# A skewness kernel: cubes written over their squares in PSUM, the sums of GpSimd's cubes in four steps, and a shorter last act for VectorE

**Chip and metric.** One core of a Trainium2 chip. The metric is the device time of one execution in microseconds (us). The engines are TensorE (PE, with its weight loads as PEld), VectorE (DVE), ScalarE (ACT), GpSimd (POOL) and SyncE (SP, which issues the loads).

## The reference

```python
x = randn(1024, 8192)            # float32
mean = np.mean(x, axis=-1, keepdims=True)
std = np.std(x, axis=-1, keepdims=True)
z = (x - mean) / (std + 1e-8)
return np.mean(z ** 3, axis=-1)
```

For each of 1024 rows the kernel needs three sums over 8192 columns: of x, of its squares, and of its cubes. The skewness follows from these.

## The kernel before

Eight blocks of 128 rows pass through, each cut into units of columns (33.55 MB of input in all, 31 loads). For each unit, PE transposes chunks of 128 columns and adds them up in PSUM (`tp`), which gives the sum of x; ACT squares and sums the squares on the way; DVE multiplies the squares by x and sums the cubes. In three places GpSimd takes the multiplication instead. The operation used there gives no sum with it, so the sum of its cubes goes round by PE (transposes into `gps`), ACT (a copy to `gsb`), PE (a product with ones, `p3`) and ACT (a copy into `s3u`).

```python
POOL = {(6, 0): 1024, (7, 0): 1024, (7, 2): 1024}   # (block, unit): columns for GpSimd
EARLY_AT = (7, 3)                                   # where blocks 0 to 6 are finished
...
tp = psum1.tile([P, P], FP, tag="tp", name="tp")
misc = psum1.tile([P, 2 * P], FP, tag="misc", name="misc")
gps = misc[:, 0:P]                    # transposes of GpSimd's cubes
s1ps = misc[:, P : P + NB]            # the mean of each block
...
def sum_cubes(sq, col):               # a generator: one step in each of several units
    for c in range(n):
        nc.tensor.matmul(out=gps, lhsT=sq[:, c * P : (c + 1) * P], rhs=ident, ..., is_transpose=True)
    yield
    nc.scalar.copy(out=gsb, in_=gps)
    p3 = misc[:, P + NB : P + NB + 1]
    nc.tensor.matmul(out=p3, lhsT=gsb, rhs=ones, start=True, stop=True)
    yield
    nc.scalar.copy(out=s3u[:, col : col + 1], in_=p3)
...
for each unit:                        # i counts the units
    # PE: transposes of xt into tp
    if last_unit:
        nc.scalar.copy(out=tsb, in_=tp)
    for s, e, on_pool in _plan(b, k):
        act(out=sq, in_=xt[:, s:e], func=AF.Square, scale=s_scale, accum_out=s2u[:, j : j + 1])
        if on_pool:
            g.tensor_tensor(out=sq, in0=sq, in1=xt[:, s:e], op=ALU.mult)
            steps = sum_cubes(sq, j)
            later += [(i + 3, steps), (i + 4, steps), (i + 5, steps)]
        else:
            nc.vector.scalar_tensor_tensor(
                out=cube[:, 0 : e - s] if (b, k) >= PSUM_FROM else sq,   # cube: one buffer in SBUF
                in0=sq, scalar=1.0, in1=xt[:, s:e],
                op0=ALU.mult, op1=ALU.mult, accum_out=s3u[:, j : j + 1])
    for at, steps in later:           # the steps that are due in this unit
        if at == i:
            next(steps, None)
    if (b, k) == EARLY_AT:
        nc.scalar.copy(out=m1a, in_=s1ps[:, 0:F])
        close_first_blocks()
# after the units of a block: tsb <- tp on ACT (but in the last block), then on PE
    nc.tensor.matmul(out=s1ps[:, b : b + 1], lhsT=tsb, rhs=onesn, start=True, stop=True)
...
# the end of the last block
g.tensor_tensor(out=m2, in0=m2p, in1=s2u[:, j - 1 : j], op=ALU.add)
act(out=m1sq, in_=p1, func=AF.Square)                        # p1: the mean, in PSUM
g.tensor_tensor(out=var, in0=m2, in1=m1sq, op=ALU.subtract)
g.tensor_tensor(out=rr, in0=var, in1=expo[:, 0:1], op=ALU.pow)
act(out=nm1, in_=p1, func=AF.Copy, scale=-3.0)
act(out=v3, in_=m1sq, func=AF.Identity, scale=1.0 / 3.0, bias=var)
nc.vector.tensor_reduce(out=num, in_=s3u[:, L * K : L * K + n_sl[L]], axis=X_AXIS, op=ALU.add)
nc.vector.scalar_tensor_tensor(out=num, in0=v3, scalar=nm1, in1=num, op0=ALU.mult, op1=ALU.add)
nc.vector.tensor_tensor(out=skew[:, L:NB], in0=num, in1=rr, op=ALU.mult)
```

In the last steps `v3` is the variance plus a third of the squared mean, `rr` the variance to the power -1.5, and `num` the numerator of the skewness. From unit 3 of block 5 on (`PSUM_FROM`) the squares lie in PSUM, in three buffers (`psq`); before that, squares and cubes share four buffers in SBUF (`sq`).

## Time and profile before

| | before |
|---|---|
| time, median of 3 runs | 93.35 us (93.28 to 93.52) |
| profiled span | 91.6 us |
| busy: PE, DVE, ACT, POOL | 75%, 78%, 76%, 12% |
| loads | 33.55 MB, 366 GB/s over the span |

A line of the timeline gives start and duration in us, engine, source line, operation, output and input, shape, count, and in brackets the idle time before it with what ended that; a line `...` marks lines left out. A square or cube that also sums (`accum_out`) is followed by a short instruction that reads out the sum, its accumulator read. Three moments: when the load stream thins out (from about 81.5 us; the last load lands near 84), when PE's last transpose ends (87.16), and when DVE's last step ends (89.36).

### The profile page before, as it was taken

Reading aid. Unit: us, or ns where it says so; the run is one execution under the profiler, and the core shown is the slowest. Engines: PE = TensorE matmul, PEld = TensorE weight load, DVE = VectorE, ACT = ScalarE, POOL = GpSimd, SP = SyncE. Lnnn points to the kernel's source line nnn. Section 1 sums busy time; section 2 is a strip of 40 time slices with the busy share of each in tenths; the row PEclk is TensorE's granted clock in tenths of the full one; section 3 lists DMA queues with packets and bytes.
Section 4 is the critical chain, followed back from the end, with each engine's and each line's share of the span. In section 5 each row is a group of like instructions: output and inputs, shape, how many; then the busy total and the mean of one; then the engine's idle time right before and its main releaser. Section 6 shows DMA issues by size and latency. Waiting matters only on the chain.

```text
span 91.6 us, 1528 instructions
## 1 busy us (share of the span) xinstructions
PE 68.9 (75%) x558; PEld 64.8 (71%) x558; DVE 71.7 (78%) x94; ACT 70.1 (76%) x117; POOL 11.3 (12%) x20
## 2 busy tenths in 40 slices
PE   0002999896983999899939796979787998977920
PEld 0003999795972999799939685969676997967910
DVE  1000498989899398999999999998999999668970
ACT  6003969696982959999949896999978998969750
POOL 3000000000000000000000000000072002998040
PEclk9999999999999569999999999999999999999999
DMA  4899999999999999999999999999999999980000
GB/s 114 329 422 422 436 436 443 408 451 422 436 415 429 416 427 429 424 405 443 417 430 404 432 423 414 416 403 422 420 415 404 411 406 409 393 319 35 0 0 2
DMA packets 4615, 33.64 MB, mean 367 GB/s; under 512 B 641, under 2 KB 769, under 8 KB 2817
## 3 DMA queue, kind: packets, MB, share of 16 engines
q1 hardware_dynamic: 4608, 33.56, 88.5%
q8 instruction: 4, 0.07, 0.3%
q14 instruction: 3, 0.02, 0.0%
HBM read 33.55 MB, written 0.00 MB: 366 GB/s over the span
## 4 chain that ended last, share of the span: by engine, by line
DMA 65%; PE 18%; ACT 5%; DVE 5%; issue 2%; SPq 1%; POOL 0%; ACTq 0%; DVEq 0%
DMA x<-in_x_dram 65%; PE tp L163 14%; DVE sq L186 5%; PE misc L140 3%; ACT sq L177 2%; ACT psq L177 2%; SPq L159 1%; PE misc L147 1%; PE misc L206 0%; ACT v_l L219 0%; ACT tsb L205 0%; DVE num_l L221 0%; POOL var_l L216 0%; POOL m_l L214 0%; ACT nm1a L127 0%
## 5 line engine op out<-in xcount | busy, mean ns | idle before, releaser
L163 PE MATMUL tp<-ident,x 128*128 128x128 f32 x512 | 63.8, 285 | 14.4 <-DMA x<-in_x_dram 14.4
L163 PEld LDWEIGHTS tp<-ident,x 128*128 128x128 f32 x512 | 60.1, 149 | 16.1 <-issue 8.5
L186 DVE SCALAR_TENSOR_TENSOR sq<-sq,x 128x2048 f32<-128x2048 f32 (+7 forms) x26 | 52.4, 2064 | 13.0 <-ACT sq L177 13.0
L177 ACT ACTIVATE sq<-x 128x2048 f32<-128x2048 f32 (+7 forms) x26 | 44.8, 1725 | 14.0 <-DMA x<-in_x_dram 14.0
L186 DVE SCALAR_TENSOR_TENSOR cube<-psq,x 128x1024 f32<-128x1024 f32 (+4 forms) x17 | 18.2, 1068 | 3.5 <-ACT psq L177 2.4
L182 POOL TENSOR_TENSOR gsq<-gsq,x 128x1024 f32<-128x1024 f32 x3 | 7.1, 2375 | 73.6 <-ACT gsq L177 73.6
L177 ACT ACTIVATE psq<-x 128x1024 f32<-128x1024 f32 (+4 forms) x17 | 15.2, 893 | 0.8 <-DMA x<-in_x_dram 0.8
L206 PEld LDWEIGHTS misc<-onesn,tsb 128*128 128x128 f32 x16 | 2.4, 188 | 5.5 <-ACT tsb L205 4.9
L206 PE MATMUL misc<-onesn,tsb 128*128 128x1 f32 x16 | 3.1, 260 | 3.6 <-ACT tsb L205 3.2
L177 ACT ACTIVATION_READ_ACCUMULATOR sq<-x 128x1 f32 x26 | 4.8, 185 | 0.0
L177 ACT ACTIVATION_READ_ACCUMULATOR psq<-x 128x1 f32 x17 | 3.2, 189 | 0.0
L177 ACT ACTIVATE gsq<-x 128x1024 f32<-128x1024 f32 x3 | 3.2, 1054 | 0.0
L140 PE MATMUL misc<-ident,gsq 128*128 128x128 f32 x24 | 3.1, 274 | 0.0
L205 ACT COPY tsb<-tp 128x128 f32<-128x128 f32 x7 | 1.8, 256 | 1.3 <-PE tp L163 1.1
L140 PEld LDWEIGHTS misc<-ident,gsq 128*128 128x128 f32 x24 | 2.7, 141 | 0.1
L186 DVE DVE_READ_ACCUMULATOR sq<-sq,x 128x1 f32 x26 | 2.2, 83 | 0.0
L147 PEld LDWEIGHTS misc<-ones,gsb 128*128 128x128 f32 x6 | 0.9, 189 | 1.4 <-ACT gsb L145 1.4
L92 ACT ACT_TABLE_LOAD x1 | 1.3, 1283 | 0.7 <-PEq L240 0.7
L147 PE MATMUL misc<-ones,gsb 128*128 128x1 f32 x6 | 1.0, 244 | 1.0 <-ACT gsb L145 1.0
L133 POOL TENSOR_TENSOR rra<-vara,expo 128x7 f32<-128x7 f32 x1 | 1.5, 1508 | 0.0
L186 DVE DVE_READ_ACCUMULATOR cube<-psq,x 128x1 f32 x17 | 1.4, 84 | 0.0
L145 ACT COPY gsb<-misc 128x128 f32<-128x128 f32 x3 | 0.8, 251 | 0.4 <-PE misc L140 0.4
(37 smaller groups left out, 7.6 us busy)
## 6 DMA issues: line engine op xcount, KB each, us to landing
x<-in_x_dram SPq DMA_DIRECT2D x6, 2048.0 KB, 18.7
x<-in_x_dram SPq DMA_DIRECT2D x7, 512.0 KB, 7.9
x<-in_x_dram SPq DMA_DIRECT2D x2, 1408.0 KB, 23.8
x<-in_x_dram SPq DMA_DIRECT2D x2, 960.0 KB, 14.6
x<-in_x_dram SPq DMA_DIRECT2D x1, 1792.0 KB, 34.4
x<-in_x_dram SPq DMA_DIRECT2D x1, 1536.0 KB, 27.8
x<-in_x_dram SPq DMA_DIRECT2D x2, 768.0 KB, 16.2
x<-in_x_dram SPq DMA_DIRECT2D x3, 448.0 KB, 10.0
```

What stands on the lines that cost most here:

```text
L92: nc.scalar.activation(out=tiny, in_=onesn, func=AF.Square)
L133: g.tensor_tensor(out=rr, in0=var, in1=expo, op=ALU.pow)
L140: nc.tensor.matmul(out=gps, lhsT=sq[:, c * P : (c + 1) * P], rhs=ident, start=c == 0, stop=c == n - 1, is_transpose=True,)
L145: nc.scalar.copy(out=gsb, in_=gps)
L147: nc.tensor.matmul(out=p3, lhsT=gsb, rhs=ones, start=True, stop=True)
L159: nc.sync.dma_start(out=xt, in_=xv[b, :, c0 : c0 + w])
L163: nc.tensor.matmul(out=tp, lhsT=xt[:, c * P : (c + 1) * P], rhs=ident, start=(k == 0 and c == 0), stop=(c0 == C and c == n - 1), is_transp ...
L177: act(out=sq, in_=xt[:, s:e], func=AF.Square, scale=s_scale, accum_out=s2u[:, j : j + 1],)
L182: g.tensor_tensor(out=sq, in0=sq, in1=xt[:, s:e], op=ALU.mult)
L186: nc.vector.scalar_tensor_tensor(out=cube[:, 0 : e - s] if (b, k) >= PSUM_FROM else sq, in0=sq, scalar=1.0, in1=xt[:, s:e], op0=ALU.mult, ...
L205: nc.scalar.copy(out=tsb, in_=tp)
L206: nc.tensor.matmul(out=s1ps[:, b : b + 1], lhsT=tsb, rhs=onesn, start=True, stop=True)
```

## The change

Its intent is to take waits out of the last 15 us: the wait of one cube for the one before, PE's wait for ACT's copy `gsb`, and two of three last steps on DVE.

```diff
-    cube = small("cube", PS_MAX)
...
         nc.scalar.copy(out=gsb, in_=gps)
+        yield
         p3 = misc[:, P + NB : P + NB + 1]
...
-                    later += [(i + 3, steps), (i + 4, steps), (i + 5, steps)]
+                    later += [(i + n, steps) for n in (3, 4, 5, 6)]
...
-                        out=cube[:, 0 : e - s] if (b, k) >= PSUM_FROM else sq,
+                        out=sq,
...
-            if b == L and k == len(widths) - 2:
+            if b == L and k == len(widths) - 3:
...                                                  # the row sum of squares, one unit earlier
+    g.tensor_tensor(out=m2p, in0=m2p, in1=s2u[:, j - 2 : j - 1], op=ALU.add)
     g.tensor_tensor(out=m2, in0=m2p, in1=s2u[:, j - 1 : j], op=ALU.add)
...
-    nc.vector.tensor_reduce(out=num, in_=s3u[:, L * K : L * K + n_sl[L]], axis=X_AXIS, op=ALU.add)
-    nc.vector.scalar_tensor_tensor(
-        out=num, in0=v3, scalar=nm1, in1=num, op0=ALU.mult, op1=ALU.add
+    n3 = small("n3_l", 1)
+    act(out=junk[:, 0 : n_sl[L] - 1], in_=s3u[:, L * K : j - 1], func=AF.Copy, accum_out=n3)
+    act(out=num, in_=v3, func=AF.Identity, scale=nm1, bias=n3)
+    nc.vector.tensor_scalar(
+        out=skew[:, L:NB], in0=s3u[:, j - 1 : j], scalar1=num, scalar2=rr,
+        op0=ALU.add, op1=ALU.mult,
     )
-    nc.vector.tensor_tensor(out=skew[:, L:NB], in0=num, in1=rr, op=ALU.mult)
```

More of the change, by code (lines that the diff above doesn't have):

```diff
@@ L198 @@
                 close_first_blocks()
-            if b == L and k == len(widths) - 2:
+            if b == L and k == len(widths) - 3:
                 m2p = small("m2p", 1)
-                act(out=junk[:, 0 : n_sl[L] - 1], in_=s2u[:, L * K : j], func=AF.Copy,
+                act(out=junk[:, 0 : n_sl[L] - 2], in_=s2u[:, L * K : j], func=AF.Copy,
                     accum_out=m2p)
```

## The prediction

> **What bounds the kernel now.** I read, in this order: the slices of the page (is the input stream saturated, and until when), the chain that ended last, the waits by engine, and the timeline of the last 20 us. The whole run took 93.35 us, the profiled span is 91.6; so 1.75 us lie outside the span, and I take them as fixed.
>
> The page's slices, each 2.29 us wide:
>
> ```profile
> PE   0002999896983999899939796979787998977920
> DVE  1000498989899398999999999998999999668970
> ACT  6003969696982959999949896999978998969750
> DMA  4899999999999999999999999999999999980000
> ```
>
> The DMA row stands at 9 from slice 3 to slice 35, that is until about 80 us, and the stretch from 64 to 81 us has a DMA share of 1.01 to 1.03. So no engine's saving can shorten the run before 80 us unless more bytes per second can be had, and a queue that is already full gives none. What is left is a tail of some 11 us in which the last units pass through PE, ACT and DVE. All three look nearly full there, so the order of waits decides. The timeline of the before kernel, PE alone (start, duration, engine, line, operation, output and input, shape, count, idle before and who ended it):
>
> ```profile
> 74.91 0.96 PE L163 MATMUL tp<-ident,x 128*128 128x128 f32 x7
> 76.28 0.38 PE L206 MATMUL misc<-onesn,tsb 128*128 128x1 f32 x2 [0.41 <-ACT tsb L205]
> 76.53 3.69 PE L163 MATMUL tp<-ident,x 128*128 128x128 f32 x32
> 80.06 1.04 PE L140 MATMUL misc<-ident,gsq 128*128 128x128 f32 x8
> 80.93 1.04 PE L163 MATMUL tp<-ident,x 128*128 128x128 f32 x8
> 82.97 0.38 PE L147 MATMUL misc<-ones,gsb 128*128 128x1 f32 x2 [1.01 <-ACT gsb L145]
> 83.21 1.07 PE L163 MATMUL tp<-ident,x 128*128 128x128 f32 x8
> ```
>
> The reader sees PE running without a gap from 76.28, except for one stall of 1.01 us at 82.97: the small matmul that adds up GpSimd's cubes (L147) stands in PE's queue ahead of the next unit's transposes and waits for a copy (gsb) that ACT does only after a square. PE's last transpose ends at 87.16, ACT's copy of it gates the last square at 87.34, and the chain goes on from there. The end, same timeline, ACT, GpSimd and DVE:
>
> ```profile
> 87.34 0.50 ACT L177 ACTIVATE psq<-x 128x384 f32<-128x384 f32 x1
> 87.77 0.19 ACT L177 ACTIVATION_READ_ACCUMULATOR psq<-x 128x1 f32 x1
> ...
> 88.53 0.29 ACT L219 ACTIVATE v_l<-m1sq_l,var_l 128x1 f32<-128x1 f32 x1 [0.38 <-POOL var_l L216]
> 88.58 0.56 POOL L217 TENSOR_TENSOR rr_l<-var_l,expo 128x1 f32<-128x1 f32 x1
> ...
> 88.88 0.22 DVE L221 SCALAR_TENSOR_TENSOR num_l<-v_l,nm_l,num_l 128x1 f32<-128x1 f32 x1
> 89.20 0.16 DVE L224 TENSOR_TENSOR skew<-num_l,rr_l 128x1 f32<-128x1 f32 x1
> ```
>
> From the end of the last square's accumulator (87.96) to the end of the last DVE step (89.36) it takes 1.40 us, and two things arrive almost together: GpSimd's power rr (89.14) and DVE's num (89.10).
>
> **What the Trainium skill says.** "PSUM — Partial Sum Buffer", Specifications, allows VectorE to read and write PSUM with 4-byte elements and to take one tensor from it, so a cube written over its square is legal; it puts ScalarE's writes to PSUM as the faster, and the trace agrees (1024 columns: 1.02 us to PSUM, 1.05 us to SBUF). It gives no time for a VectorE write to PSUM, and no line here has one. "VectorE: DVE Perf Modes", The DRAIN you can't avoid, says a semaphore between two VectorE operations costs nothing extra. The trace disagrees: after a cube in SBUF (sq) the next one starts as the accumulator read starts (both 66.47), after one into the single buffer "cube" it starts 0.17 to 0.19 us later (read 67.34, next 67.53). "ScalarE: Activation LUTs", What ACT_TABLE_LOAD costs, gives about 93 ns for each per-partition pointer operand of an ACTIVATE; the trace has 0.17 us for a one-column one with none and 0.29 for v3 with one, so about 0.12 each.
>
> **The change part by part.**
>
> (1) Cubes over their squares. The write after write on "cube" goes, and with it the 0.18 us before 16 of 17 cubes: 2.9 us on DVE. From 66.5 to 78.0 DVE is back to back and behind ACT, so there it catches up (some nine gaps, 1.6 us) and frees its inputs earlier: the queue's own waits give 8.8 us in 7 waits on these cubes. But the loads they release join a full queue. After 78 us DVE waits for ACT before its cubes (0.29, 0.84, 0.89 and 0.39 us), so it isn't the bound there either. Worth to the end: about 0 in itself, but it keeps DVE off the path once PE and ACT come earlier: cubes of the last four units end about 0.7 us sooner than they would.
>
> (2) The copy and the small matmul come in two units instead of one. For the first GpSimd unit, PE's transposes that now start at 74.91 no longer stand behind the small matmul and start near 74.65; they end near 75.6 instead of 75.87, ACT's copy (tsb, 75.96 now, after 0.36 of waiting) comes when ACT is free, near 75.65. That shifts everything behind it by 0.3: the squares of the last block, GpSimd's multiplications and PE's 32 transposes. For the second one, at 82.97 before: PE passes directly from the 8 transposes ending near 81.6 to the 8 of the next unit (landed: issued 75.74, 5.7 to 5.8 us to landing, so 81.5), ends them near 82.55, and then meets the small matmul, for which gsb is there at 82.6. So the stall of 1.01 shrinks to about 0.1. From 82.65 on PE has, by the starts of the same pieces: matmul 0.24, 8 transposes 0.94, 7 transposes 0.83, 6 transposes 0.71, matmul 0.2, 3 transposes 0.35: 3.27, and 0.1 of latency, ends at 86.0. Before 87.16: **1.15 us earlier**. ACT, with the copies that it does in this stretch only moved, ends its last but one square near 85.8 and isn't later than PE. The last square starts near 86.2 and its accumulator is read at 86.8 (87.96 before).
>
> (3) The end. GpSimd has one more addition (0.19 us), but it needs the last but one square only, and lies before the last one. Its chain of three steps stays: 87.96 to 89.14 before is 1.18. ACT now does v3 (starts 0.57 after the accumulator, ends 0.86), then the sum of the cubes (0.21 and a read of 0.19 that starts 0.11 in, as with the other row sum at 86.45 and 86.56; begun some 0.2 after v3's start, done near 1.07), then num with two pointer operands (about 0.29 + 0.12 = 0.41, from 1.10 to 1.51), then one DVE step (0.06 and about 0.2). That ends 1.75 us after the accumulator, where it was 1.40: **0.35 us later**. What DVE gives up (0.16 + 0.22 + 0.16) was partly beside GpSimd's power, so taking it away buys little, while ACT's two new steps stand in line.
>
> (4) The row sum of the squares comes one unit earlier: 0.3 us of ACT moved from before the last square, where ACT waited 0.43 for PE, to a place where it is full; next to nothing.
>
> Sum: -1.15 + 0.35 = -0.80 of 91.6, so 93.35 - 0.80 = **92.55 us**.
>
> **The rivals.** (a) *DVE's saving is the big one*: 2.9 us of gaps gone, earlier loads, a run of 90.5 to 91.5. For it: DVE has the largest busy time (78%) and the load queue waits for it longest. Against: a DMA share of 1.02 while it does so, and idle DVE after 78 us. 6 in 100. (b) *VectorE is slow when it reads and writes the same PSUM bank*: the 14,848 columns of these cubes at 1.04 ns would take 15.5 us more if the rate halved, and DVE, which has under 6 us of slack and gaps, would become the bound: over 100 us. Nothing in the trace speaks for it and nothing excludes it, since no such instruction is there. A mild form, some 50 ns more for each cube, would hide. 5 in 100. (c) *The end eats the gain*: ACT's two new steps wait for each other and for semaphores, and cost 0.8 rather than 0.35: 93.0. (d) *The stall only moves*: PE meets gsb as late as before, because ACT waits for the first-block copy (0.73 us, m1a) in both kernels; half the gain of 1.15 is 0.57, and with 0.35 for the end that gives 93.1. For it: ACT, not PE, sets when gsb is there. Against: one unit's transposes (0.94 us) now lie in that wait. (e) *The data of the next units is not there*: a transfer landing at 81.5 is needed at 81.6; a delay of 0.3 would cost as much.
>
> **The range and the chances.** (c), (d) and (e) each take up to half a microsecond away; (a) in a weak form, a last load that lands earlier, may add as much. So 91.9 to 93.2 holds it 8 times in 10. Faster by over 2% needs 91.48 or less, which only (a) gives: 0.07. Slower by over 2% needs 95.2, which only (b) gives: 0.05. Within 2%: 0.88.
>
> **What would show it.** Right: the next cube starting with the accumulator read of the one before; cubes still 1.22 us for 1024 columns; no PE wait over 0.3 us at L147; PE's last transpose near 86.0; the end 1.7 to 1.8 us after the last accumulator of squares. Wrong: cubes longer than 1.3 us at 1024 columns, a stall of PE of another kind between 80 and 86 us, a DMA share well above or a stream that ends more than 1 us earlier, or an end of 1.4 or of over 2 us.

## The result

The changed kernel took **93.28 us** (median of 4 runs, 93.17 to 93.32), the kernel before, in 4 runs, 93.36. The ratio is 0.9987 (95% interval 0.9969 to 1.0004): the same. A ratio here is the mean time of one kernel's fast runs over that of the other's in the same rounds, so not quite the ratio of the medians. The prediction was 92.55 (91.9 to 93.2): the class was right, the time missed, with the measured value just above the range.

Where did the expected 0.8 us go? First PE, in the timeline of the changed kernel:

```profile
80.74 1.91 PE L163 MATMUL tp<-ident,x 128*128 128x128 f32 x16
82.78 0.38 PE L147 MATMUL misc<-ones,gsb 128*128 128x1 f32 x2
...
85.49 0.52 PE L163 MATMUL tp<-ident,x 128*128 128x128 f32 x3
86.94 0.38 PE L206 MATMUL misc<-onesn,tsb 128*128 128x1 f32 x2 [0.92 <-ACT s3u L149]
```

The stall of 1.01 us ahead of L147 no longer shows: sixteen transposes run in a row and the small matmul follows (its weight load still waits 0.37 us for `gsb`). The last transpose ends at 85.49 + 0.52 = 86.01, where the prediction had 86.0 and the kernel before 87.16. So PE gained its 1.15 us. The new thing is the last line: the matmul of the last mean (L206) waits 0.92 us for ACT's copy into s3u (L149), which it did not do before. The same three steps in the kernel before, where the copy came before the last square:

```profile
86.31 0.15 ACT L149 COPY s3u<-misc 128x1 f32<-128x1 f32 x1
...
87.50 0.38 PE L206 MATMUL misc<-onesn,tsb 128*128 128x1 f32 x2 [0.36 <-ACT tsb L169]
...
87.92 0.17 ACT L215 ACTIVATE m1sq_l<-misc 128x1 f32<-128x1 f32 x1
```

Now the end, ACT, POOL and DVE of the changed kernel's timeline:

```profile
86.22 0.50 ACT L177 ACTIVATE psq<-x 128x384 f32<-128x384 f32 x1
86.64 0.19 ACT L177 ACTIVATION_READ_ACCUMULATOR psq<-x 128x1 f32 x1
86.73 0.15 ACT L149 COPY s3u<-misc 128x1 f32<-128x1 f32 x1
...
87.36 0.17 ACT L216 ACTIVATE m1sq_l<-misc 128x1 f32<-128x1 f32 x1 [0.47 <-PE misc L206]
...
87.67 0.19 POOL L217 TENSOR_TENSOR var_l<-m_l,m1sq_l 128x1 f32<-128x1 f32 x1 [0.50 <-ACT nm_l L219]
87.89 0.29 ACT L220 ACTIVATE v_l<-m1sq_l,var_l 128x1 f32<-128x1 f32 x1 [0.30 <-POOL var_l L217]
...
88.09 0.19 ACT L223 ACTIVATE junk<-s3u 128x8 f32<-128x8 f32 x1
...
88.41 0.39 ACT L224 ACTIVATE num_l<-v_l,n_l,nm_l 128x1 f32<-128x1 f32 x1
88.90 0.27 DVE L225 TENSOR_SCALAR skew<-s3u,num_l,rr_l 128x1 f32<-128x1 f32 x1 [1.32 <-ACT num_l L224]
```

The last square's accumulator is read by 86.83, 1.13 us earlier than before (87.96). But from there to DVE's end (89.17) it takes 2.34 us, and in the kernel before 1.40. Two parts make up these 0.94 us:

| from the last accumulator | before | changed | longer by |
|---|---|---|---|
| to the start of v3 | 88.53 - 87.96 = 0.57 | 87.89 - 86.83 = 1.06 | 0.49 |
| start of v3 to DVE's end | 89.36 - 88.53 = 0.83 | 89.17 - 87.89 = 1.28 | 0.45 |

In the first part, the copy of GpSimd's last sum now comes a unit later, behind the last square. The matmul of the mean writes another column of the same PSUM tile (`misc`) and does not start before that copy has read its own; I take the shared tile for the reason. The mean's square (87.36) thus comes 0.53 us after the accumulator, where it came before the accumulator's end. In the second part, ACT's sum of the cubes and num stand in line behind v3.

The cubes themselves did as forecast. DVE in the kernel before, then in the changed kernel, three lines of the timeline each:

```profile
75.76 1.09 DVE L186 SCALAR_TENSOR_TENSOR cube<-psq,x 128x896 f32<-128x896 f32 x1
76.78 0.08 DVE L186 DVE_READ_ACCUMULATOR cube<-psq,x 128x1 f32 x1
76.95 1.09 DVE L186 SCALAR_TENSOR_TENSOR cube<-psq,x 128x896 f32<-128x896 f32 x1
```

```profile
74.87 1.13 DVE L186 SCALAR_TENSOR_TENSOR psq<-psq,x 128x896 f32<-128x896 f32 x1
75.92 0.14 DVE L186 DVE_READ_ACCUMULATOR psq<-psq,x 128x1 f32 x1
75.92 1.13 DVE L186 SCALAR_TENSOR_TENSOR psq<-psq,x 128x896 f32<-128x896 f32 x1
```

The next cube now starts with the accumulator read of the one before. From one 896-column cube to the next it takes 75.92 - 74.87 = 1.05 us instead of 76.95 - 75.76 = 1.19: 0.14 us less. The gap of 0.17 us is gone, but a cube takes 0.03 us longer up to its own accumulator read (1.05 against 1.02); the read that now runs beside its start also grew, from 0.08 to 0.14 us, which may be why. And hardly any of it moved the loads: the last one was issued at 79.3 us instead of 79.8, and landed near 84 as before. The DMA row of the changed kernel's slices:

```profile
DMA  4899999999999999999999999999999999981000
```

### The profile page after: what moved, and what is told of

Its sections match the earlier page's. It is cut to its first block, busy times and chain, and to the rows that moved or that the text cites. A ratio compares the mean times of both kernels' runs of the same rounds, so it can differ in the third digit from the quotient of the medians.

```text
span 91.4 us, 1526 instructions
## 1 busy us (share of the span) xinstructions
PE 68.3 (75%) x558; PEld 63.9 (70%) x558; DVE 70.9 (78%) x92; ACT 70.4 (77%) x120; POOL 11.5 (13%) x21
## 4 chain that ended last, share of the span: by engine, by line
DMA 71%; DVE 9%; ACT 7%; PE 5%; issue 3%; SPq 1%; POOL 0%; DVEq 0%; ACTq 0%
DMA x<-in_x_dram 71%; DVE sq L186 5%; DVE psq L186 4%; PE tp L163 4%; ACT psq L177 3%; ACT sq L177 2%; PE misc L139 1%; SPq L159 1%; PE misc L206 0%; ACT num_l L224 0%; ACT v_l L220 0%; DVE skew L225 0%; ACT junk L223 0%; POOL var_l L217 0%; ACT m1sq3a L125 0%
## 5 line engine op out<-in xcount | busy, mean ns | idle before, releaser
L163 PE MATMUL tp<-ident,x 128*128 128x128 f32 x512 | 63.1, 282 | 14.9 <-DMA x<-in_x_dram 14.8
L163 PEld LDWEIGHTS tp<-ident,x 128*128 128x128 f32 x512 | 59.1, 147 | 17.2 <-DMA x<-in_x_dram 8.9
L186 DVE SCALAR_TENSOR_TENSOR psq<-psq,x 128x1024 f32<-128x1024 f32 (+4 forms) x17 | 17.7, 1093 | 2.9 <-ACT psq L177 2.9
L206 PEld LDWEIGHTS misc<-onesn,tsb 128*128 128x128 f32 x16 | 2.4, 188 | 5.8 <-ACT tsb L205 4.6
L206 PE MATMUL misc<-onesn,tsb 128*128 128x1 f32 x16 | 3.1, 260 | 4.0 <-ACT tsb L205 3.1
L186 DVE DVE_READ_ACCUMULATOR psq<-psq,x 128x1 f32 x17 | 2.4, 140 | 0.0
L147 PEld LDWEIGHTS misc<-ones,gsb 128*128 128x128 f32 x6 | 0.9, 190 | 0.4 <-ACT gsb L144 0.4
L147 PE MATMUL misc<-ones,gsb 128*128 128x1 f32 x6 | 0.9, 226 | 0.1
```

The costliest lines, as they stand in the source:

```text
L163: nc.tensor.matmul(out=tp, lhsT=xt[:, c * P : (c + 1) * P], rhs=ident, start=(k == 0 and c == 0), stop=(c0 == C and c == n - 1), is_transp ...
L186: nc.vector.scalar_tensor_tensor(out=sq, in0=sq, scalar=1.0, in1=xt[:, s:e], op0=ALU.mult, op1=ALU.mult, accum_out=s3u[:, j : j + 1],)
```

## The experiments

Twelve kernels ran, each in five rounds beside the kernel before. **The theory** after the result: PE's gain is real, and two separate losses at the end eat it, a new wait (the mean behind the copy, 0.49 us) and a longer line (0.45 us). **The rivals**: only the longer line counts, and the wait ends beside other work; only the larger of the two counts; or DVE and its cubes in PSUM hold the end.

| run | what it is | median us | ratio to before (95%) |
|---|---|---|---|
| the change | all parts | 93.28 | 0.9987 (0.9969 to 1.0004) |
| e1_copy_first | change, copy ahead | 92.85 | 0.9954 (0.9938 to 0.9970) |
| e2_old_end | change, old last steps | 92.84 | 0.9945 (0.9931 to 0.9958) |
| e3_both | change, both edits | 92.46 | 0.9912 (0.9896 to 0.9928) |
| e4_new_end_only | before, new last steps | 93.72 | 1.0050 (1.0031 to 1.0068) |
| e5_psum_only | before, cubes in PSUM | 93.43 | 1.0009 (0.9996 to 1.0022) |
| e6_four_steps_only | before, four steps | 93.02 | 0.9966 (0.9954 to 0.9979) |
| e7_both_sbuf | e3, cubes in SBUF | 92.94 | 0.9959 (0.9946 to 0.9971) |
| e8_less_pool | e3, one cube to DVE, late closing | 91.75 | 0.9834 (0.9820 to 0.9847) |
| e9_sum_ahead | e1, ACT's sum ahead of v3 | 92.51 | 0.9920 (0.9907 to 0.9934) |
| e10_pool_only | e3, one cube to DVE | 92.36 | 0.9906 (0.9893 to 0.9920) |
| e11_close_later_only | e3, late closing | 91.85 | 0.9850 (0.9837 to 0.9864) |
| e12_less_pool_one_step | e8, ACT's sum ahead, one DVE step | 91.62 | 0.9829 (0.9816 to 0.9842) |

Runs e1 to e4 were taken together (before: 93.35), so were e5 to e8 (93.31) and e9 to e12 (93.23); the change itself was timed apart from all of them. Across these groups I compare the ratios.

### e1_copy_first: the copy ahead of the last unit's work

```diff
             if last_unit:
+                for at, steps in later:
+                    if at == i:
+                        next(steps, None)
+                later = [z for z in later if z[0] > i]
                 nc.scalar.copy(out=tsb, in_=tp)
```

> The changed kernel with one edit: ACT's last copy of GpSimd's cube sum (s3u, L149) is issued ahead of the last unit's transposed copy (tsb) instead of behind the last square. Theory (a new wait: PE's last mean matmul L206 stands 0.92 us behind that copy): L206 starts near 86.4 instead of 86.94, the mean's square follows the last square's accumulator within 0.1 us, and the run ends 0.45 to 0.5 us earlier than the changed kernel: 92.8. Rival (the wait at L206 ends beside GpSimd's or DVE's work, the longer line of ACT steps alone holds the end): within 0.1 us of the changed kernel, 93.2 to 93.3.

Measured: 92.85 us, as the theory said. Its timeline:

```profile
86.41 0.38 PE L210 MATMUL misc<-onesn,tsb 128*128 128x1 f32 x2 [0.35 <-ACT tsb L173]
...
86.83 0.17 ACT L220 ACTIVATE m1sq_l<-misc 128x1 f32<-128x1 f32 x1
...
88.02 0.39 ACT L228 ACTIVATE num_l<-v_l,n_l,nm_l 128x1 f32<-128x1 f32 x1
88.51 0.27 DVE L229 TENSOR_SCALAR skew<-s3u,num_l,rr_l 128x1 f32<-128x1 f32 x1 [0.89 <-ACT num_l L228]
```

The matmul of the mean (now L210) starts at 86.41 instead of 86.94 and waits only for `tsb`; the mean's square comes at 86.83, with the accumulator. The wait was on the path, and its cause is the place of one 0.15 us copy in ACT's queue. That the two collide because they share a PSUM tile or bank is how I read it and is not shown: a tile of its own for `p3` was not tried.

### e2_old_end: the three old last steps on DVE

```diff
-    n3 = small("n3_l", 1)
-    act(out=junk[...], in_=s3u[:, L * K : j - 1], func=AF.Copy, accum_out=n3)
-    act(out=num, in_=v3, func=AF.Identity, scale=nm1, bias=n3)
-    nc.vector.tensor_scalar(...)
+    nc.vector.tensor_reduce(...); nc.vector.scalar_tensor_tensor(...); nc.vector.tensor_tensor(...)
```

> The changed kernel with the last steps of the kernel before (sum of cubes, multiply and add, multiply: three on DVE) in place of ACT's two new steps and the one DVE step; the copy stays behind the last square. Theory (the new line is 0.45 us longer than the old one from the start of v3: 1.28 against 0.83): 92.85, with v3 still 1.06 us behind the end of the last square's accumulator. Rival (DVE, now with the cubes right ahead of it, cannot run three steps any sooner than ACT did): no change, 93.3.

Measured: 92.84 us, as the theory said. Its timeline:

```profile
87.93 0.29 ACT L220 ACTIVATE v_l<-m1sq_l,var_l 128x1 f32<-128x1 f32 x1 [0.30 <-POOL var_l L217]
...
88.58 0.16 DVE L225 TENSOR_TENSOR skew<-num_l,rr_l 128x1 f32<-128x1 f32 x1
```

From v3's start to the end it is 88.74 - 87.93 = 0.81 us, against 1.28 with the new steps. v3 is still late: the last accumulator is read by 86.87, and v3 comes 1.06 us later. So the two losses are separate.

### e3_both: both edits

The two diffs above together, on the changed kernel.

> Both edits: the copy ahead, and the old last steps. Theory: both losses are separate and add up, so the 1.15 us that PE gained show whole: 92.35, with 1.4 us from the last square's accumulator to the end as in the kernel before. Rival (only one of the two waits ends last, so taking both away gives no more than the larger): 92.8.

Measured: 92.46 us. By the ratios the copy ahead gives 0.31 us and the old end 0.39, each of them the same alone and on top of the other (by the medians 0.38 to 0.44), so both were on the path, one after the other, and the "only the larger" rival falls. Against the predicted 92.35, 0.1 us is missing. The DVE lines of its timeline tell why:

```profile
86.84 0.60 DVE L190 SCALAR_TENSOR_TENSOR psq<-psq,x 128x384 f32<-128x384 f32 x1
...
87.53 0.16 DVE L225 TENSOR_REDUCE num_l<-s3u 128x1 f32<-128x9 f32 x1
87.81 0.22 DVE L226 SCALAR_TENSOR_TENSOR num_l<-v_l,nm_l,num_l 128x1 f32<-128x1 f32 x1
```

v3 is ready at 87.67, but DVE is only then done with its sum of cubes (87.69), behind a last cube that starts as soon as the one before lets it. DVE has become a second bound.

### e4_new_end_only: the new last steps in the kernel before

```diff
-    nc.vector.tensor_reduce(...); nc.vector.scalar_tensor_tensor(...); nc.vector.tensor_tensor(...)
+    act(out=junk[...], in_=s3u[:, L * K : j - 1], func=AF.Copy, accum_out=n3)
+    act(out=num, in_=v3, func=AF.Identity, scale=nm1, bias=n3)
+    nc.vector.tensor_scalar(...)
```

> The kernel before with ACT's two new steps and the one DVE step at the end, nothing else. Theory: the new end is longer by 0.45 us in itself, 93.8. Rival (the new end is no longer, it is only the late mean that makes it so): 93.35.

Measured: 93.72 us, ratio 1.0050, so 0.47 us slower. The lines:

```profile
88.39 0.29 ACT L219 ACTIVATE v_l<-m1sq_l,var_l 128x1 f32<-128x1 f32 x1 [0.37 <-POOL var_l L216]
...
88.91 0.39 ACT L223 ACTIVATE num_l<-v_l,n_l,nm_l 128x1 f32<-128x1 f32 x1
89.39 0.27 DVE L224 TENSOR_SCALAR skew<-s3u,num_l,rr_l 128x1 f32<-128x1 f32 x1 [0.97 <-ACT num_l L223]
```

89.66 - 88.39 = 1.27 us from v3 to the end. The new end is a loss in itself, without the other parts of the change. DVE now sits idle for 0.97 us ahead of its one step, and GpSimd's power has ended at 89.00.

### e5_psum_only: only the cubes over their squares

```diff
-                        out=cube[:, 0 : e - s] if (b, k) >= PSUM_FROM else sq,
+                        out=sq,
```

> The kernel before with the cubes written over their squares in PSUM, nothing else. Theory (DVE off the path there, a full load queue): 93.35 within 0.1 us, with some 0.14 us less between the starts of cubes in a row. Rival (DVE frees inputs earlier, loads come earlier): 92.5 or less.

Measured: 93.43 us, ratio 1.0009. DVE's gaps went and nothing else did. Alone this part gives nothing; if anything the longer accumulator read of the last cube (0.14 instead of 0.08 us), with the sum of cubes 0.06 us later behind it, shows at the end; the interval includes no difference.

### e6_four_steps_only: only the four steps

```diff
         nc.scalar.copy(out=gsb, in_=gps)
+        yield
...
-                    later += [(i + 3, steps), (i + 4, steps), (i + 5, steps)]
+                    later += [(i + n, steps) for n in (3, 4, 5, 6)]
```

> The kernel before with the sums of GpSimd's cubes in four steps, nothing else. Theory (PE gains 1.15 us, the mean waits 0.49 us for the copy behind the last square, and DVE, still with its gaps, ends its last cube near 88.1 where the last steps want it at 88.2): 92.8 to 92.95. Rival (without the cubes in PSUM, DVE is late and holds the end): 93.2 or more.

Measured: 93.02 us, ratio 0.9966: 0.32 us faster, a little outside the forecast. PE's last transpose ends at 85.96, so its gain is whole; the mean waits 0.92 us for the copy, as forecast. But DVE, still with a gap ahead of each cube, ends the last one at 88.02 and starts its multiply-and-add at 88.41, while v3 ended at 88.13. Part of the rival is true: DVE is late by about 0.2 us.

### e7_both_sbuf: the e3 kernel with the cubes back in SBUF

```diff
-                        out=sq,
+                        out=cube[:, 0 : e - s] if (b, k) >= PSUM_FROM else sq,
```

> The better kernel of the runs before (copy ahead, old last steps) with the cubes back in their one buffer in SBUF. Theory (the gaps of 0.14 to 0.18 us before the last cubes put DVE on the path once PE and ACT are early: last cube near 88.1 instead of 87.45): 93.0. Rival (DVE stays off the path, writing to PSUM is worth nothing in any company): 92.46, as with them in PSUM.

Measured: 92.94 us, ratio 0.9959, against 0.9912 for e3: 0.44 us slower. Its DVE lines stand against those of e3:

```profile
87.57 0.56 DVE L191 SCALAR_TENSOR_TENSOR cube<-psq,x 128x384 f32<-128x384 f32 x1
...
88.17 0.16 DVE L226 TENSOR_REDUCE num_l<-s3u 128x1 f32<-128x9 f32 x1
```

The last cube starts 0.73 us later than in e3, 0.15 of it because ACT and PE are that much later in this profile too. So the same edit is worth nothing in the kernel before and 0.44 us where PE and ACT have been made early. The rival that the cubes in PSUM hold the end falls with this: taking them out costs time.

### e8_less_pool, e10_pool_only, e11_close_later_only: beyond both kernels

```diff
-POOL = {(6, 0): 1024, (7, 0): 1024, (7, 2): 1024}
+POOL = {(6, 0): 1024, (7, 0): 1024}                  # e8 and e10, on e3
-EARLY_AT = (7, 3)
+EARLY_AT = (7, 4)                                    # e8 and e11, on e3
```

> A version beyond both kernels: copy ahead, old last steps, and two edits more: GpSimd's cube of unit 2 of the last block goes to DVE (which waits 2.7 us for ACT after 77 us), which takes 8 transposes and a matmul (1.18 us) off PE's tail; the first blocks are closed one unit later, so that ACT doesn't wait 0.81 us for PE. Theory (PE then ends near 84.7, ACT and DVE follow within 0.3 us): 91.5. Rival (DVE with one cube more, or the last load landing near 84.0, holds the end): 92.2 or more.

> The 92.46 us kernel (copy ahead, old last steps) with GpSimd's cube of unit 2 of the last block given to DVE, nothing else. Theory (PE loses 1.18 us of its tail, but ACT, which still waits 0.8 us for PE before the last five squares, becomes the bound after 0.3 to 0.4 us): 92.1. Rival (PE alone held the end): 91.75, as with both edits.

> The 92.46 us kernel with the first blocks closed one unit later, nothing else. Theory (ACT gets 0.8 us of slack, but PE holds the end and gains only the 0.1 us for which it waited for gsb): 92.3 to 92.4. Rival (ACT's wait of 0.8 us for PE is on the path): 91.7.

Measured: 91.75, 92.36 and 91.85 us. The pair came 0.25 us short of what I expected (91.5), and I had the shares wrong: in e11 the rival (91.7) was the nearer. The edit of GpSimd's cube, forecast as 0.36 us, gives 0.06 alone (0.9906 against 0.9912), which is within the intervals; closing the first blocks one unit later, forecast as about 0.1, gives 0.58 (0.9850 against 0.9912). On top of that, GpSimd's cube for DVE gives 0.15 us (0.9834 against 0.9850), again with intervals that overlap. The lines of e11:

```profile
80.11 1.03 ACT L181 ACTIVATE psq<-x 128x1024 f32<-128x1024 f32 x1
...
82.35 0.28 PE L147 MATMUL misc<-ones,gsb 128*128 128x1 f32 x2
...
85.53 0.27 ACT L173 COPY tsb<-tp 128x128 f32<-128x128 f32 x1 [0.23 <-PE tp L163]
```

With the closing later, ACT doesn't wait 0.81 us for PE and starts that square at 80.11 instead of 81.36. Two things follow. The copy gsb comes early, so PE's small matmul starts at 82.35 instead of 82.69 and the 8 transposes behind it at 82.50 instead of 82.94: in e3 PE was still held there by 0.4 us, of which I had seen 0.1. And DVE's last five cubes start earlier (81.29 instead of 82.53), which lifts the second bound as well. In e10 ACT's last accumulator comes 0.28 us earlier than in e3 (86.47 against 86.75), near the forecast, but DVE's last cube starts at 86.86 as in e3 (86.84), because its row of five cubes hangs on the same late square. The e10 forecast took ACT for the bound and missed DVE.

### e9_sum_ahead and e12_less_pool_one_step: the new last steps, better placed

```diff
+    n3 = small("n3_l", 1)
+    act(out=junk[...], in_=s3u[:, L * K : j - 1], func=AF.Copy, accum_out=n3)
     act(out=v3, in_=m1sq, func=AF.Identity, scale=1.0 / 3.0, bias=var)
-    n3 = small("n3_l", 1)
-    act(out=junk[...], in_=s3u[:, L * K : j - 1], func=AF.Copy, accum_out=n3)
```

The diff is that of e9, on e1. The kernel e12 is the changed kernel with this edit, the copy ahead (e1) and the two lines shown for e8.

> The changed kernel with the copy ahead (which ran in 92.85 us), and ACT's sum of the cubes issued ahead of v3, into the 0.44 us in which ACT waits for GpSimd's var, instead of behind v3. Theory (0.2 us of the longer end is that sum standing between v3 and num): num starts right behind v3, 92.65. Rival (num waits for v3 or for rr just as long): 92.85. What would be left against the old last steps (92.46) is num's two pointer operands, 0.39 us on ACT against 0.22 on DVE.

> The 91.75 us kernel with ACT's sum (ahead of v3) and num and the one DVE step in place of the old last steps. Theory (in that kernel DVE's last cube, ending 0.7 us later after the last square than before, holds the old last steps; one DVE step needs only the cube itself): 91.65, so that the change's own last part pays once DVE is the bound. Rival (num's 0.39 us on ACT holds the end): 91.85 or more.

Measured: 92.51 us (ratio 0.9920, e1: 0.9954) and 91.62 us (ratio 0.9829, e8: 0.9834). In e9 num follows v3 at once:

```profile
87.32 0.29 ACT L226 ACTIVATE v_l<-m1sq_l,var_l 128x1 f32<-128x1 f32 x1
...
87.65 0.39 ACT L228 ACTIVATE num_l<-v_l,n_l,nm_l 128x1 f32<-128x1 f32 x1
```

In e1 num started 0.52 us after v3 did, here 0.33: 0.19 us of the longer end were the sum standing in line, in time in which ACT had nothing to do a moment earlier. The ratio moved by 0.32 us, with an interval of some 0.2 on either side, so the other 0.13 may be noise. e12, the fastest kernel here, is 1.7% faster than the kernel before; against e8 its gain (0.05 us) is within the intervals. In the two profiles the one DVE step neither gains nor loses: from the end of the last square's accumulator read to the end it is 1.84 us in both (85.82 to 87.66 in e8, 85.69 to 87.53 in e12). In e8 num starts 0.42 us after v3's end, held by DVE's last cube; in e12 ACT's sum waits 0.38 us for a cube of DVE, and the one DVE step 0.53 us for num. So the forecast 91.65 was met, but its reason is not shown.

## Why the prediction was wrong

- **What bounds the kernel**: right. The load stream stayed full to the same moment, and the time was made in the tail. (Its 1.75 us outside the span set the median against the span of another run; the profiled run took 93.47 us, so 1.87, and 1.84 in the changed kernel. They are fixed, as it assumed.)
- **Part 1, cubes over squares**: right as stated. e5 shows no gain alone, and the clause that it "keeps DVE off the path once PE and ACT come earlier" is what e7 measured as 0.44 us. The gain per cube was 0.14 us, not 0.18, and its 16 gaps (2.9 us) were 12 (some 2.1): four of the cubes start after a wait for ACT, as its own text lists.
- **Part 2, PE**: right in its sum (85.49 + 0.52 = 86.01 against 86.0), with some luck. The small matmul started at 82.78, not 82.65, and from there PE took 3.23 us, not 3.27 and 0.1: two errors of about 0.13 that cancel. Ahead of it the transposes of the last block came 0.47 us earlier (76.06 against 76.53), not 0.3, and were down to 0.20 at 79.86, after a wait of 0.30 us for a load: a little of rival (e). The stall was not cut to 0.1 us either; e11 shows that 0.4 us of it were left. Rival (d), that the stall partly moves, had that much of truth.
- **Part 3, the end: this is the step that failed.** It said "0.35 us later" and it was 0.94. Of the error of 0.59 us, 0.10 is size: the term from v3 to the end grew by 0.45 rather than 0.35 (DVE's step began 0.10 us after num's end and took 0.27, where 0.06 and about 0.2 stood, and its own terms add up to 1.77, not 1.75). The other 0.49 is a wait that no step of the prediction had: it put v3 at 0.57 us after the accumulator as before, and did not ask what else had moved into ACT's queue. "ACT, with the copies that it does in this stretch only moved" names the very copies; one of them had moved behind the last square, and the matmul of the mean behind it. e1 shows the cost. Its list of signs had named this case as wrong: "an end of 1.4 or of over 2 us"; the end was 2.34. Its 0.12 us for each pointer operand came from a step that reads PSUM (0.17) against one that reads SBUF (0.29). Steps of ACT on SBUF alone take 0.19 with none (seven columns), 0.29 with one (v3) and 0.39 with two (num), so 0.10 each, close to the 93 ns that it cites from "ScalarE: Activation LUTs".
- **Part 4**: nothing is seen of it, as said, though no run has it alone. In e6, which keeps the old row sum, ACT's copy `tsb` starts 0.04 us after the last transpose, as in the changed kernel.
- **Rival (c)**, that the end eats the gain, was the right one, for half of the right reason. With part 3 at 0.94, the prediction's own sum is -1.15 + 0.94 = -0.21; the span shows 91.6 to 91.4, the timed runs 0.08 to 0.12 us.

A warning of the missing wait was in the Trainium skill, "PSUM — Partial Sum Buffer", PSUM bank collisions raise a hardware error: "Semaphore-guard PSUM by **bank × quadrant** (by bank is the simple version), not by address." The trace of the kernel before has a wait that fits it:

```profile
81.13 0.17 ACT L197 COPY m1a<-misc 128x7 f32<-128x7 f32 x1 [0.73 <-PE misc L140]
```

ACT's copy m1a, which reads the means in `misc`, waits 0.73 us for transposes (L140) that write other columns of `misc`. I had read that line as an ordinary wait. Whether the bank or the tile is what is guarded here, no run tells.

## What to carry to other kernels

When steps are spread over more units, follow the last one of them to where it now lands: behind the last big operation it can hold something else, above all if both touch one PSUM tile. Count the last chain as a line of dependent steps, each with its own cost (0.16 to 0.56 us for one column here), and not by which engine is relieved; work that can be done while the chain waits belongs ahead of it in the queue. And a saving on an engine that isn't the bound can be worth nothing alone and 0.4 us next to another, so try it again once the bound has moved.

## What the Trainium skill lacked or had wrong

- "VectorE: DVE Perf Modes", The DRAIN you can't avoid, says of eight tensor copies in a row that "the semaphore costs nothing extra here". That does not carry over to these cubes, which also sum: a cube whose output is the one buffer of the cube before started 0.17 to 0.19 us after the accumulator read began, and with rotating buffers together with it; from start to start that was 1.19 against 1.05 us at 896 columns. How much of it is the semaphore's, the trace does not show.
- "PSUM — Partial Sum Buffer", Specifications, gives no time for VectorE in place in PSUM, and no other page that I found has one. Reading and writing the same buffer went at the same rate as with the output in SBUF (1024 columns: 1.24 us on average against 1.23), and the accumulator read behind it took 0.14 instead of 0.08 us.
- "Vector Engine (DVE) Microarchitecture Reference", 7. Points that are easy to get wrong, says that this operation with two sources in SBUF that are not bf16 has half the throughput; of what, it does not say. Against the same operation with one source in PSUM it was not so here: with both sources float32 in SBUF 1408 columns took 1.62 us and 2048 took 2.29, so 0.67 us for 640 columns or 1.05 ns each; with one source in PSUM, from 896 columns (1.09) to 1024 (1.23), it was (1.225 - 1.092) / 128 = 1.04 ns.
